# TensorE's order in the experts of a gated-DeltaNet, MLA and MoE block: written out by hand instead of left to the scheduler, with four token buffers and the final gain row loaded by DMA

## The chip, the cores and the metric

The kernel runs on one core of a Trainium2 chip. The metric is the device time of one execution in microseconds (us), the median of several executions. The profile is of one further execution, in which the hardware profiler recorded every instruction and every DMA packet.

## What is computed

One encoder block on 512 tokens of width 1024 in float32: two token mixers, their merge, and a mixture of 16 experts in which each expert picks its 64 best tokens. Cut to the part around the change, the reference is:

```python
def expert_choice_ffn(h, w_router, w_gate, w_up, w_down):
    cap = 64                                   # 2 * 512 // 16
    aff = softmax(h @ w_router)                # 512 x 16
    gate, idx = lax.top_k(aff.T, cap)          # each expert picks its tokens
    xe = h[idx]                                # 16 x 64 x 1024
    hid = silu(xe @ w_gate) * (xe @ w_up)      # each weight 1024 x 1024 per expert
    ye = (hid @ w_down) * gate
    return zeros_like(h).at[idx].add(ye)       # scattered back onto the tokens

x = x + gt2 * expert_choice_ffn(rms_norm(x, g_ffn) * (1 + sc2) + sh2, ...)
return rms_norm(x, g_final)
```

The gate, up and down weights of the 16 experts are 48 matrices of 4 MiB, 201 MB in all, each read once from HBM.

## The kernel before

The first two thirds of the program (both token mixers, their merge, the router with its top-64 selection) are not touched. The experts follow, from about 850 us on.

**Weights.** Each expert has three matrices m = 0 (gate), 1 (up), 2 (down), each cut into four quarters of 128 x 2048 floats. `order()` lists them as gate of e, down of e-1, up of e, for one expert after another; at the end stand gate and up of expert 15, down of expert 14 and down of expert 15, the last cut by columns into five pieces (three of 256 columns, two of 128; `last`). `load_quarters` (L988) issues their DMAs on SP in that order into a ring of 17 buffers `exw`; a quarter can be issued once TensorE has read the quarter 17 places before it.

**One expert.** `products(m, e, of)` runs the gate or up quarters: a quarter is four instructions in the program's order (two 128-row slices, two 64-column halves of the array) and eight records in the trace; they write the PSUM tiles `wg` and `wu`. `activated(e)` makes silu(gate) x up x score (ScalarE L1475, VectorE L1476). `turned(e)` transposes it on TensorE (tile `hTp`, L1482) and ScalarE copies it out. `down(e)` multiplies by the down quarters (tile `dnp`), and VectorE multiplies by the modulation row `gt2` into `ye` (L1505).

**Gather.** Tokens are gathered with one-hot matrices, four experts (a group) at a time: `group(g)` builds the one-hot `OG` on VectorE, and `gather(g, j0, n)` multiplies it by the token slices, which are split into a high and a low half (`xh` on ScalarE, `xl` on GpSimd); 16 matmuls for a pair of slices. The result goes to `XE[g]`, one tile `xe` of eight slices.

**Scatter.** `scatter(i, ye)` adds the outputs of a pair of experts i onto the tokens: for two column halves it splits `ye` into `yh` and `yl`, and for each of four token blocks runs two matmuls with the transposed one-hot `OHT` (made by `rows(i)`) into one of two PSUM tiles `sc`; VectorE adds the tile to the tokens (L1452). Eight such tiles a scatter. `gates(i)` collects a pair's scores with eight small matmuls.

**Order.** Up to the end of expert 14 the order of TensorE's instructions is set by the scheduler, from the order of the calls in the loop; the loop issues the scatter of the pair before, then `rows`, `group`, then the next expert's gate quarters, `turned`, `down` and the up quarters:

```python
        if e % 2 == 0 and i:
            scatter(i - 1, ye)
        if e % 4 == 3:
            group(e // 4 + 1)
        products(0, e + 1, range(3))
        turned(e)
        products(0, e + 1, [3])
        if e < NE - 2:
            down(e)
        products(1, e + 1)
```

**End.** The row `g_final` is loaded as 1 x 1024 and spread over the partitions by two matmuls with a row of ones (`spread`, L1318). Then come down of expert 14, and the five pieces of down of expert 15 in an order that is written by hand for TensorE, VectorE and ScalarE: matmuls of a piece, scatter of the piece before, adds, squares (`summed`), and GpSimd's multiplication by g_final (L1563, 16 instructions). After the last piece the row sums `rq` give the scale, and the tokens are scaled and stored.

Of the kernel before, what the change touches and what calls it, by code (L numbers as in the profile page):

```python
# [13 lines left out]
AF = mybir.ActivationFunctionType  # L14
# [8 lines left out]
NE = 16  # L23
# [17 lines left out]
def block_kernel(ctx: ExitStack, tc: tile.TileContext, x, c, positions, w_mod, b_mod, g_mix, w_in, conv_w,  # L41
# [1320 lines left out]
    def group(g):  # L1362

        o = wk_("OG", [4, 4, 64], F32R)
        e4 = slt[:, :, 4 * g:4 * g + 4][:, :, :, None].to_broadcast([128, 4, 4, 64])
        for h in (slice(0, 2), slice(2, 4)):
            dve.tensor_tensor(o[:, h], iot[:, None, None, :].to_broadcast([128, 2, 4, 64]), e4[:, h], op=OP.is_equal)
        XE[g] = wk_("xe", [8, 256])
        OG[g] = o
        if g:  # L1370
            for j in range(0, 8, 2):
                gather(g, j, 2)

    def gather(g, j0, n):

        ps = bank("mm")
        for j in range(n):
            hl_ = ahead.pop(j0 + j, None) if g == 0 else None
            hl_ = hl_ or halves_of(j0 + j)
            for t in range(4):  # L1380
                for v in range(2):
                    mm(ps[:, 256 * j:256 * j + 256], hl_[v][:, t], OG[g][:, t].rearrange("p e c -> p (e c)"),
                       t == 0 and v == 0, t == 3 and v == 1)
        for j in range(n):
            k = j0 + j
            a, b, v = sh_g[1][:, k:k + 1], sh_g[0][:, k:k + 1], ps[:, 256 * j:256 * j + 256]
            if k % 2:
                act.activation(XE[g][:, k, :], v, AF.Identity, bias=b, scale=a)
            else:
                dve.tensor_scalar(XE[g][:, k, :], v, a, b, op0=OP.mult, op1=OP.add)  # L1390

    def onehot(i):

# [59 lines left out]

    yb = []
    ssq = wk_("ssq3", [4, 5])
# [3 lines left out]
    def products(m, e, of=range(4)):  # L1459

        s_ = slice(64 * (e % 4), 64 * (e % 4) + 64)
        if (m, e) not in hid:
            hid[m, e] = bank(("wg", "wu")[m], 1, pe_)
        for hf in of:
            w = quarter(m, e, hf)
            for j in range(2 * hf, 2 * hf + 2):
                for q in range(2):
                    done = mm(hid[m, e][64 * q:64 * q + 64, :], XE[e // 4][:, j, s_],
                              w[:, j % 2].rearrange("p (a h b) -> p h a b", h=2, b=4)[:, q], j == 0, j == 7)
        return done  # L1470

# [6 lines left out]
    def turned(e):  # L1478
# [4 lines left out]
        hT_[e] = late[:, 0:512] if e == NE - 2 else wk_("sg_", 512)  # L1483
        act.activation(hT_[e], ps, AF.Copy)

    def lhid(e):
        return lambda j: hT_[e][:, 128 * (j % 4) + 64 * (j // 4):128 * (j % 4) + 64 * (j // 4) + 64]

    def down(e, middle=None):

        o_, lh, ps = slice(64 * (e % 2), 64 * (e % 2) + 64), lhid(e), bank("dnp", 1, pe_)
        for hf in range(4):
            if hf == 2 and middle:
                middle()
            w = quarter(2, e, hf)
            for j in range(2 * hf, 2 * hf + 2):
                for q in range(2):
                    done = mm(ps[64 * q:64 * q + 64, :], lh(j), w[:, j % 2, 512 * q:512 * q + 512], j == 0, j == 7)
        if e == 0:
            with tc.issue_after(done.ins):  # L1500
                spread(gt2, 0)
# [10 lines left out]
        done = products(m, 0, [hf])  # L1512
    gates(0)

    for e in range(NE - 1):
        i = e // 2
# [12 lines left out]
        turned(e)  # L1529
        products(0, e + 1, [3])  # L1530
        if e % 2 == 0:
            ye = wk_("ye", 1024)
# [9 lines left out]
    down(NE - 2, lambda: turned(NE - 1))  # L1542
# [3 lines left out]
    ctx.enter_context(tc.manual_schedule(engines={pe.engine, dve.engine, act.engine}))  # L1546

    def square(c, t, on):

# [88 lines left out]
```

## Time and profile before

| | |
|---|---|
| median of 3 runs | 1327.65 us (1326.37 to 1330.58) |
| the profiled execution's own time | 1334.39 us |
| its span, first to last instruction | 1332.5 us |
| mean granted TensorE clock | 0.977 of full |
| TensorE busy (matmul) | 1246.2 us, 94% |
| VectorE / ScalarE / GpSimd busy | 681.4 / 480.4 / 306.5 us |
| DMA moved | 333.17 MB, mean 250 GB/s |

The profiled execution took 1.9 us more than its span and 6.7 us more than the median of the runs. Busy shares are averages over stages with different limits; a table by stretches of time is read for the stage that the change touches. In the rows further down, PE is TensorE's matmuls, DVE VectorE, ACT ScalarE, POOL GpSimd, SP the queue that issues most DMAs; clock 1.00 is 2.4 GHz, 0.50 is 1.2 GHz.

### The profile page before, as it was taken

The numbers are of one execution on the slowest core, as the hardware profiler recorded it, in microseconds if no ns is written. First come the engines' busy times: TensorE is split into PE (matmuls) and PEld (weight loads), VectorE is DVE, ScalarE is ACT, GpSimd is POOL, SyncE is SP. The second block draws the span as 40 slices with busy tenths as digits, with TensorE's granted clock in tenths as the row PEclk, the third lists the DMA queues.
The fourth block names the chain that finished last, engine by engine and source line by source line (L and its number), as shares of the span: only waits on it lengthen the run. The fifth ranks groups of instructions, "written<-read, shape, count | busy, mean of one in ns | idle before, by whom it ended". The sixth has DMA issues, their size and how long they took to land.

```text
span 1332.5 us, 18305 instructions
## 1 busy us (share of the span) xinstructions
PE 1246.2 (94%) x6937; PEld 781.4 (59%) x6937; DVE 681.4 (51%) x1312; ACT 480.4 (36%) x993; POOL 306.5 (23%) x259
## 2 busy tenths in 40 slices
PE   6999999999998897999999999699999999999995
PEld 3767777666676675878877777333443443343334
DVE  4687766365679896535586766412131122212125
ACT  4466554456543334444542336411200110110013
POOL 2321200323444242444222243200200200110003
PEclk9999999999999898999999999799999999999998
DMA  9421213744453566677579673799999999999992
GB/s 352 140 60 44 80 48 99 234 138 135 138 162 96 173 166 187 181 231 187 175 250 333 221 288 127 288 380 421 420 420 421 420 421 420 421 420 421 421 388 76
DMA packets 153364, 333.17 MB, mean 250 GB/s; under 512 B 44545, under 2 KB 104143, under 8 KB 128316
## 3 DMA queue, kind: packets, MB, share of 16 engines
q1 hardware_dynamic: 129906, 308.23, 62.9%
q10 hardware_dynamic: 23034, 23.36, 5.6%
q8 instruction: 55, 0.90, 0.3%
q0 software_dynamic: 336, 0.41, 0.2%
q14 instruction: 33, 0.27, 0.1%
HBM read 307.83 MB, written 24.13 MB: 249 GB/s over the span
## 4 chain that ended last, share of the span: by engine, by line
PE 69%; DVE 16%; issue 5%; DMA 5%; ACT 3%; POOL 1%; SPq 0%; DVEq 0%; ACTq 0%; POOLq 0%
PE mm L88 23%; PE wg L88 9%; PE dnp L88 8%; PE wu L88 6%; PE po L88 5%; DVE pr L783 3%; PE lat L88 3%; PE sc L88 2%; DVE lanT L784 2%; PE s L88 2%; DMA wraw<-in_w_in_dram 1%; PE I L88 1%; PE pja L88 1%; PE S L88 1%; PE V L88 1%
## 5 line engine op out<-in xcount | busy, mean ns | idle before, releaser
L88 PE MATMUL mm<-hT,wh 128*128 128x512 f32 (+1 forms) x672 | 223.3, 409 | 0.0
L96 POOL TENSOR_TENSOR wl<-wraw,wh 128x512 fp32r<-128x512 f32 (+2 forms) x83 | 119.0, 1448 | 262.6 <-ACT wh L99 250.1
L88 PEld LDWEIGHTS mm<-hT,wh 128*128 128x128 f32 (+1 forms) x672 | 125.4, 190 | 44.2 <-issue 10.5
L99 ACT ACTIVATE wh<-wraw 128x512 fp32r<-128x512 f32 (+1 forms) x139 | 87.1, 650 | 137.8 <-PE mm L88 55.0
L88 PE MATMUL mm<-hT,wl 128*128 128x512 f32 (+1 forms) x336 | 135.7, 404 | 0.0
L88 PE MATMUL wg<-exw,xe 128*64 128x512 f32 x512 | 124.3, 603 | 1.3 <-DVE xe L1390 1.3
L1505 DVE TENSOR_TENSOR ye<-dnp,gt 64x512 f32<-64x512 f32 x30 | 20.7, 688 | 201.0 <-PE dnp L88 185.1
L88 PE MATMUL wu<-exw,xe 128*64 128x512 f32 x512 | 118.1, 596 | 0.0
L96 POOL TENSOR_TENSOR xl<-xs,xh 128x512 fp32r<-128x512 f32 x32 | 40.4, 1272 | 322.2 <-ACT xh L1358 258.1
L88 PEld LDWEIGHTS wu<-exw,xe 128*64 128x64 f32 x512 | 35.4, 137 | 67.0 <-issue 62.2
L88 PEld LDWEIGHTS mm<-hT,wl 128*128 128x128 f32 (+1 forms) x336 | 63.6, 189 | 15.8 <-DVE wl L96 0.6
L88 PEld LDWEIGHTS wg<-exw,xe 128*64 128x64 f32 x512 | 34.3, 137 | 58.9 <-issue 49.8
L96 DVE TENSOR_TENSOR wl<-wraw,wh 128x512 fp32r<-128x512 f32 (+1 forms) x56 | 47.2, 848 | 33.1 <-ACT wh L99 32.2
L783 DVE TENSOR_TENSOR pr<-lanT,nl 128x1 f32<-128x1 f32 (+30 forms) x62 | 56.7, 914 | 1.7
L1452 DVE TENSOR_TENSOR xa<-sc,xa 128x512 f32<-128x512 f32 x56 | 36.4, 686 | 31.2 <-PE sc L88 31.0
L88 PE MATMUL po<-W,am 128*128 128x512 f32 x192 | 50.1, 405 | 0.6 <-DVE W L96 0.6
L1358 ACT ACTIVATE xh<-xs 128x512 fp32r<-128x512 f32 x32 | 20.1, 629 | 70.6 <-PE sc L88 36.0
L660 DVE SCALAR_TENSOR_TENSOR cv<-mm,vecT,cv 128x510 f32<-128x510 f32 (+1 forms) x32 | 23.9, 748 | 39.7 <-ACT cv L656 39.1
L88 PE MATMUL mm<-oz,wh 128*128 128x512 f32 x128 | 40.3, 398 | 0.5 <-ACT wh L99 0.5
L88 PE MATMUL mm<-am,wh 128*128 128x512 f32 x128 | 40.7, 398 | 0.0
L88 PEld LDWEIGHTS po<-W,am 128*128 128x128 f32 x192 | 34.6, 188 | 10.4 <-issue 1.6
L1563 POOL TENSOR_TENSOR xa<-xa,late 128x256 f32<-128x256 f32 (+1 forms) x16 | 10.4, 686 | 118.2 <-ACT exw L1555 118.2
(599 smaller groups left out, 2435.5 us busy)
## 6 DMA issues: line engine op xcount, KB each, us to landing
exw<-in_w_gate_dram SPq DMA_DIRECT2D x64, 1024.0 KB
exw<-in_w_up_dram SPq DMA_DIRECT2D x64, 1024.0 KB
exw<-in_w_down_dram SPq DMA_DIRECT2D x63, 1024.0 KB
wraw<-in_w_in_dram SPq DMA_DIRECT2D x38, 512.0 KB
wm<-in_w_mod_dram SPq DMA_DIRECT2D x32, 512.0 KB
wraw<-in_w_in_dram ACTq DMA_DIRECT2D x16, 512.0 KB
xa<-in_w_mod_dram SPq DMA_DIRECT2D x16, 512.0 KB
kq<-kq_d SPq DMA_DIRECT2D x7, 1024.0 KB
```

Source lines behind the costliest of these rows:

```text
L88: return pe.matmul(o, lhsT, rhs, start=start, stop=stop)
L96: eng.tensor_tensor(o, a, b, op=OP.subtract)
L99: act.activation(hi, src, AF.Copy)
L660: dve.scalar_tensor_tensor(cv[:, -s:], ps[:, :512 + s], w(d), cv[:, -s:], op0=OP.mult, op1=OP.add)
L783: dve.tensor_tensor(pv, T3[:, 0:i, 0:i], nb, op=OP.mult)
L784: dve.tensor_reduce(T3[:, 0:i, i], pv, axis=AX.X, op=OP.add)
L1358: act.activation(xh, xs[:, j], AF.Copy)
L1452: dve.tensor_tensor(y[t][:, c:c + 512], ps, y[t][:, c:c + 512], op=OP.add)
L1505: dve.tensor_tensor(ye[o_, c], ps[64 * q:64 * q + 64, :], gt2[64 * q:64 * q + 64, c], op=OP.mult)
L1563: pool.tensor_tensor(y[t][:, cs], y[t][:, cs], gfin[:, cs], op=OP.mult)
```

## The change

TensorE's order is fixed by hand from expert 0 on. In an even iteration the eight tiles of the scatter stand one behind each quarter of the next expert's gate and of this expert's down. The gather of the next group stands, a pair of slices at a time, between the up quarters of the last expert of a group, and so `xe` becomes four tiles of two slices each, of which the first can be overwritten when the first up quarter has read it. `turned(e)` follows the third gate quarter. `rows` moves behind `down` of the even expert. The g_final row is read from HBM into all 128 partitions by one DMA of 512 KB, issued on SP behind the last piece of weights, in place of the two matmuls.

```diff
@@ group, gather
-        XE[g] = wk_("xe", [8, 256])
+        XE[g] = {}
         OG[g] = o
-        if g:
-            for j in range(0, 8, 2):
-                gather(g, j, 2)
...
+        if j0 // 2 not in XE[g]:
+            XE[g][j0 // 2] = wk_(f"xe{j0 // 2}", [2, 256])
@@ scatter
+        halves_ = []
         for c in range(0, D, 512):
             yh, yl = ...
             split(yh, yl, ye[:, c:c + 512])
+            halves_.append((c, yh, yl))
+        for c, yh, yl in halves_:
             for t in range(4):
...
                 dve.tensor_tensor(y[t][:, c:c + 512], ps, y[t][:, c:c + 512], op=OP.add)
+                yield
@@ down
-    def down(e, middle=None):
+    def down(e, between=()):
...
         for hf in range(4):
-            if hf == 2 and middle:
-                middle()
...
+            next(between, None)
@@ the loop over the experts
+    pe_order.enter_context(tc.manual_schedule(engines={pe.engine}))
     for e in range(NE - 1):
...
         activated(e)
-        if e % 2 == 0 and i:
-            scatter(i - 1, ye)
-        if e % 2 or e == NE - 2:
+        between = scatter(i - 1, ye) if e % 2 == 0 and i else iter(())
+        for k in range(4):
+            products(0, e + 1, [k])
+            next(between, None)
+            if k == 2:
+                turned(e)
+        if e < NE - 2:
+            if e % 2 == 0:
+                ye = wk_("ye", 1024)
+            down(e, between)
+        for _ in between:
+            pass
+        if e % 2 == 0:
             rows(i)
-        if e % 4 == 3:
-            group(e // 4 + 1)
-        products(0, e + 1, range(3))
-        turned(e)
-        products(0, e + 1, [3])
-        if e < NE - 2:
-            down(e)
-            if e % 2:
-                gates(i + 1)
-        products(1, e + 1)
-    sp.dma_start(gfin[0:1], g_final.rearrange("(o n) -> o n", o=1))
-    spread(gfin, 0)
-    spread(gfin, 1)
+        if e < NE - 2 and e % 2:
+            gates(i + 1)
+        if e % 4 == 2 and g < NE // 4:
+            group(g)
+        for k in range(4):
+            products(1, e + 1, [k])
+            if e % 4 == 2 and g < NE // 4:
+                gather(g, 2 * k, 2)
@@ before the five last pieces
+    load_quarters(parts.index((2, e, 0)), len(parts))
+    sp.dma_start(gfin, g_final.rearrange("(o n) -> o n", o=1).to_broadcast([128, 1024]))
```

How the rows of TensorE move. In the scatter of experts 6 and 7, before the change: `wu` are the up quarters of expert 8 (one row x4 is a quarter), `sc` the scatter's tiles.

```order
L88 MATMUL wu<-exw,xe 64x512 x4
L88 MATMUL sc<-yh,OHT 128x512
L88 MATMUL sc<-yl,OHT 128x512
L88 MATMUL sc<-yh,OHT 128x512
L88 MATMUL sc<-yl,OHT 128x512
L88 MATMUL sc<-yh,OHT 128x512
L88 MATMUL wu<-exw,xe 64x512 x4
L88 MATMUL sc<-yl,OHT 128x512
```

Two and a half tiles stand behind the first quarter, the rest behind the next ones. With the change, the same scatter (`wg` are the gate quarters of expert 9, `hTp` the transposes of expert 8):

```order
L88 MATMUL wg<-exw,xe_8712 64x512 x4
L88 MATMUL sc<-yh,OHT 128x512
L88 MATMUL sc<-yl,OHT 128x512
L88 MATMUL wg<-exw,xe_8746 64x512 x4
L88 MATMUL sc<-yh,OHT 128x512
L88 MATMUL sc<-yl,OHT 128x512
L88 MATMUL wg<-exw,xe_8780 64x512 x4
L88 MATMUL sc<-yh,OHT 128x512
L88 MATMUL sc<-yl,OHT 128x512
L1487 MATMUL hTp<-ident,sg__8937 128x128 x4
L88 MATMUL wg<-exw,xe_8814 64x512 x4
```

Each quarter now has one tile behind it (the other four stand behind the quarters of down), and the transposes have moved from the end of the up quarters to behind the third gate quarter. VectorE's rows for that scatter, with the change: `xa<-sc` are its adds, `sg` is the activation of expert 8, `ye<-dnp` the two halves of down's output.

```order
L96 TENSOR_TENSOR yl<-ye,yh 128x512 x2
L1481 SCALAR_TENSOR_TENSOR sg__8937<-wu,gate,sg__8937 128x512
L1456 TENSOR_TENSOR xa<-sc,xa 128x512 x7
L1515 TENSOR_TENSOR ye<-dnp,gt_7703 64x512
L1456 TENSOR_TENSOR xa<-sc,xa 128x512
L1515 TENSOR_TENSOR ye<-dnp,gt_7703 64x512
```

Both halves of `yl` stand ahead of the activation, and seven of the eight adds ahead of down's output. On SP, the end of the weights and the stores, with the change:

```order
L988 DMA exw<-in_w_down_dram 128x2048 x4
L988 DMA exw<-in_w_down_dram 128x8x256 x3
L988 DMA exw<-in_w_down_dram 128x8x128 x2
L1585 DMA late<-in_g_final_dram 128x1024
L1625 DMA out_dram<-xa 128x448
```

Before, g_final's row (`late<-in_g_final_dram 1x1024`) stood ahead of the four down quarters of expert 14.

## Rows read from the trace of the kernel before

**Rows 1.** Spans and granted clock of the cores.
```profile
core 0: 1332.5 us, clock 0.977
```
**Rows 2.** The page, the span in 40 slices of 33.3 us: DMA busy tenths, GB/s.
```profile
DMA  9421213744453566677579673799999999999992
GB/s 352 140 60 44 80 48 99 234 138 135 138 162 96 173 166 187 181 231 187 175 250 333 221 288 127 288 380 421 420 420 421 420 421 420 421 420 421 421 388 76
```
**Rows 3.** Busy time by stretches: PE, PEld, DVE, ACT, POOL, then clock, DMA share, GB/s.
```profile
850.00:860.00 10.00, 9.36 (x48) 5.11 (x48) 0.95 (x2) 3.25 (x6) 5.03 (x4) 0.88 0.45 165
880.00:890.00 10.00, 10.00 (x46) 3.67 (x47) 0.00 (x0) 1.16 (x2) 0.00 (x0) 1.00 0.99 413
1250.00:1260.00 10.00, 10.00 (x49) 3.43 (x50) 0.00 (x0) 0.60 (x1) 0.00 (x0) 1.00 1.01 420
```
**Rows 4.** The same view, the end of the weight stream.
```profile
1295.00:1298.00 3.00, 3.00 (x13) 1.27 (x14) 0.00 (x0) 2.75 (x4) 0.00 (x0) 0.68 1.02 315
...
1302.00:1303.00 1.00, 1.00 (x6) 0.29 (x4) 0.00 (x0) 0.00 (x0) 0.00 (x0) 1.00 0.02 4
1303.00:1304.00 1.00, 1.00 (x8) 0.29 (x4) 0.00 (x0) 0.00 (x0) 0.00 (x0) 1.00 0.00 0
```
**Rows 5.** Timeline of the end: start us, us, engine, line, operation [idle before <-releaser].
```profile
1293.12 1.98 PE L88 MATMUL mm<-late,ones 1*128 1x512 f32 x4
...
1295.71 8.78 PE L88 MATMUL dnp<-exw,late 128*64 128x512 f32 x32
...
1306.04 1.97 PE L88 MATMUL dnp<-exw,sg__9867 128*64 128x128 f32 x32 [1.54 <-issue]
...
1310.81 1.97 PE L88 MATMUL wu<-exw,sg__9867 128*64 128x128 f32 x32
...
1316.22 1.15 PE L88 MATMUL dnp<-exw,sg__9867 128*64 128x64 f32 x32
...
1323.05 0.17 DVE L1592 TENSOR_REDUCE rq<-ssq 128x4 f32<-128x20 f32 x1
```
**Rows 6.** Timeline, the same place four experts apart: up quarters begin.
```profile
1006.33 7.04 PE L88 MATMUL wu<-exw,xe 128*64 128x512 f32 x32
...
1123.84 4.46 PE L88 MATMUL wu<-exw,xe 128*64 128x512 f32 x20
```
**Rows 7.** Timeline of TensorE in one scatter (experts 6 and 7), up quarters of expert 8.
```profile
1094.51 1.89 PE L88 MATMUL wu<-exw,xe 128*64 128x512 f32 x8
...
1098.36 0.50 PE L88 MATMUL sc<-yh,OHT 128*128 128x512 f32 x1 [0.48 <-DVE xa L1452]
...
1105.57 0.50 PE L88 MATMUL sc<-yh,OHT 128*128 128x512 f32 x1 [0.32 <-DVE xa L1452]
...
1106.24 1.94 PE L88 MATMUL wu<-exw,xe 128*64 128x512 f32 x8
1108.11 0.50 PE L88 MATMUL sc<-yh,OHT 128*128 128x512 f32 x1
...
1109.03 0.63 PE L1482 MATMUL hTp<-ident,sg__8926 128*128 128x128 f32 x3 [0.19 <-DVE sg__8926 L1476]
```
**Rows 8.** Timeline of TensorE: transposes of expert 7, then the gather, which begins.
```profile
1070.19 0.75 PE L1482 MATMUL hTp<-ident,sg__8711 128*128 128x128 f32 x4 [0.91 <-DVE sg__8711 L1476]
...
1071.88 0.39 PE L88 MATMUL mm<-OG,xh 128*128 128x256 f32 x1
...
1074.10 1.08 PE L88 MATMUL wg<-exw,xe 128*64 128x512 f32 x4
```
**Rows 9.** Groups by line, 850 to 1333 us: busy us, mean ns, idle before.
```profile
L1563 POOL TENSOR_TENSOR xa<-xa,late 128x256 f32<-128x256 f32 (+1 forms) x16 | 10.4, 686 | 118.2 <-ACT exw L1555 118.2
L1600 ACT ACTIVATE xa<-xa,rq 128x896 f32<-128x896 f32 x2 | 2.0, 1034 | 0.3 <-DVE rq L1594 0.3
```
**Rows 10.** Busy time by stretches: TensorE with gaps, earlier in the program, columns of rows 3.
```profile
400.00:420.00 20.00, 16.84 (x74) 12.99 (x72) 19.55 (x31) 6.24 (x14) 8.45 (x5) 1.00 0.43 132
450.00:460.00 10.00, 7.04 (x21) 5.33 (x21) 5.80 (x11) 3.59 (x9) 4.26 (x5) 0.66 0.48 159
```

More of the change, by code (lines that the diff above doesn't have):

```diff
@@ L1367, in group @@
             dve.tensor_tensor(o[:, h], iot[:, None, None, :].to_broadcast([128, 2, 4, 64]), e4[:, h], op=OP.is_equal)
-        XE[g] = wk_("xe", [8, 256])
+        XE[g] = {}
         OG[g] = o
-        if g:
-            for j in range(0, 8, 2):
-                gather(g, j, 2)
     def gather(g, j0, n):
         ps = bank("mm")
+        if j0 // 2 not in XE[g]:
+            XE[g][j0 // 2] = wk_(f"xe{j0 // 2}", [2, 256])
+        xe = XE[g][j0 // 2]
         for j in range(n):
@@ L1387, in gather @@
             if k % 2:
-                act.activation(XE[g][:, k, :], v, AF.Identity, bias=b, scale=a)
+                act.activation(xe[:, k % 2, :], v, AF.Identity, bias=b, scale=a)
             else:
-                dve.tensor_scalar(XE[g][:, k, :], v, a, b, op0=OP.mult, op1=OP.add)
+                dve.tensor_scalar(xe[:, k % 2, :], v, a, b, op0=OP.mult, op1=OP.add)
     def onehot(i):
@@ L1467, in products @@
                 for q in range(2):
-                    done = mm(hid[m, e][64 * q:64 * q + 64, :], XE[e // 4][:, j, s_],
+                    done = mm(hid[m, e][64 * q:64 * q + 64, :], XE[e // 4][j // 2][:, j % 2, s_],
                               w[:, j % 2].rearrange("p (a h b) -> p h a b", h=2, b=4)[:, q], j == 0, j == 7)
@@ L1484, in turned, with turned_ @@
         act.activation(hT_[e], ps, AF.Copy)
+    def turned_(e):
+        yield
+        turned(e)
+        yield
     def lhid(e):
         return lambda j: hT_[e][:, 128 * (j % 4) + 64 * (j // 4):128 * (j % 4) + 64 * (j // 4) + 64]
-    def down(e, middle=None):
+    def down(e, between=()):
+        between = iter(between)
         o_, lh, ps = slice(64 * (e % 2), 64 * (e % 2) + 64), lhid(e), bank("dnp", 1, pe_)
         for hf in range(4):
-            if hf == 2 and middle:
-                middle()
             w = quarter(2, e, hf)
@@ L1513, in block_kernel @@
     gates(0)
+    pe_order = ctx.enter_context(ExitStack())
+    pe_order.enter_context(tc.manual_schedule(engines={pe.engine}))
     for e in range(NE - 1):
-        i = e // 2
+        i, g = e // 2, e // 4 + 1
         if e == NE - 2:
@@ L1521, in block_kernel @@
         activated(e)
-        if e % 2 == 0 and i:
-            scatter(i - 1, ye)
-        if e % 2 or e == NE - 2:
-            rows(i)
-        if e % 4 == 3:
-            group(e // 4 + 1)
-        products(0, e + 1, range(3))
-        turned(e)
-        products(0, e + 1, [3])
-        if e % 2 == 0:
-            ye = wk_("ye", 1024)
-        if e < NE - 2:
-            down(e)
-            if e % 2:
-                gates(i + 1)
-        products(1, e + 1)
-    sp.dma_start(gfin[0:1], g_final.rearrange("(o n) -> o n", o=1))
-    spread(gfin, 0)
-    spread(gfin, 1)
+        between = scatter(i - 1, ye) if e % 2 == 0 and i else iter(())
[3 more added lines that the diff above has]
+            if k == 2:
+                turned(e)
+        if e < NE - 2:
[5 more added lines that the diff above has]
+        if e % 2 == 0:
+            rows(i)
+        if e < NE - 2 and e % 2:
[6 more added lines that the diff above has]
+                gather(g, 2 * k, 2)
+    ye = wk_("ye", 1024)
     activated(NE - 1)
-    down(NE - 2, lambda: turned(NE - 1))
+    down(NE - 2, turned_(NE - 1))
     e, i, o_ = NE - 1, NE // 2 - 1, slice(64, 128)
@@ L1545, in block_kernel @@
     act.activation(ssq[:, 0, 0:1], lh(0)[:, 0:1], AF.Sqrt, bias=eps1, scale=0.0)
-    ctx.enter_context(tc.manual_schedule(engines={pe.engine, dve.engine, act.engine}))
+    ctx.enter_context(tc.manual_schedule(engines={dve.engine, act.engine}))
     def square(c, t, on):
```

## The prediction

> **What bounds the kernel now.** I read the table by stretches first, not the busy shares of the page. From about 880 us the DMA engines are full: 413 GB/s, then 420, at a DMA share of 0.99 to 1.01 [rows 3], and the slices show 420 or 421 GB/s without a dip for some 400 us [rows 2]. Weights are nearly all of it. Before that stretch they are not full (165 GB/s at 850 us), since TensorE frees the ring's buffers slowly while it gathers for the first group.
>
> Four experts are 48 quarters of 1.049 MB, 50.3 MB, which at 420 GB/s take 119.8 us. TensorE passes the same place four experts later after 1123.84 - 1006.33 = 117.5 us [rows 6]. So both run at nearly the same pace, and TensorE, which starts behind with a full ring, catches up by only 2.3 us in four experts. That it never has to wait for a weight does not make it the bound, and that the DMA is full does not make the DMA the bound: what decides is who is late at the end. There the answer is in two rows. The weight stream ends between 1302 and 1303 us (4 GB/s in that stretch, none after it) [rows 4], and I take 1302.7; TensorE reads the last piece at 1316.22 [rows 5]. **TensorE is 13.5 us behind the data.** So it is TensorE's path that sets the end now, and the stream is a floor 13.5 us below it.
>
> From the second stretch on, the end is a chain by itself: from the third of the five last pieces (1310.81) to the end of the span (1332.5) it takes 21.7 us, in which VectorE is the busy one, and 12.2 us of that lie ahead of the row sums at 1323.05 [rows 1, 5].
>
> **What the change is worth on TensorE's path.** A block of 32 records takes 7.04 us [rows 6], so a quarter 1.76.
>
> - *Scatter.* Now it costs the time from 1094.51 to 1109.03 less four quarters: 14.5 - 7.0 = 7.5 us [rows 7]; in it TensorE waits for VectorE's adds (0.48 and 0.32 are shown), because two or three tiles come in a row and there are two PSUM tiles. With one tile behind each quarter a tile costs 0.67 us (1105.57 to 1106.24), and a quarter with a tile behind it 1.87 instead of 1.76 (1106.24 to 1108.11), so 0.78 a tile and 6.2 a scatter. Gain 1.3 us, two scatters in four experts: 2.6. VectorE's add of a tile has more than 2 us until its PSUM tile is used again, so its wait goes under the quarters.
> - *Transposes.* In two of four experts TensorE waits 0.9 us for the activation [rows 8]; behind the third gate quarter, 5 us later, it is long ready. Gain 1.8 in four experts. ScalarE's copy of the result has the fourth gate quarter, 1.76 us, as cover; without it, down would wait for it.
> - *Gather.* 17 matmuls take 1071.88 to 1074.10, 2.2 us [rows 8], and the same number runs after the change. In pieces of 16 between quarters a piece pays the quarter's 0.11 once more. The gain is that GpSimd's split of the next pair runs under a quarter; the loss is that each pair waits for buffers of the pair before. I take 0, between -1 and +1 us a group. The four token buffers themselves cost nothing: each is overwritten right behind the quarter that read it last.
> - *Rows, gates, SP's order of weights* are the same instructions in other places: 0.
> - *g_final.* Two matmuls (1.98 us) leave the path. They use one row of the array, and right after them the clock was granted at 0.68 for three us [rows 4], so that down of expert 14 took 8.78 us where such a block takes 7.04 [rows 5, 6]. Together 3.7 us.
>
> Four experts give 4.4 us; from the third expert, where the DMA fills, to the end there are about 3.3 times four: 14.5 us, and with g_final **18 us that TensorE could be earlier**. Bounds: 3.7 if the new places gain nothing, about 25 if the waits around the gather go too. It can use only 13.5 of it, then it waits for each quarter as it lands.
>
> **What the new floor gives.** The stream has the same bytes and starts with the same gathers, so I let it end at 1302.7 again. The last two pieces, 1.05 MB at 315 GB/s [rows 4], are 3.3 us, so the third has landed at about 1299.4. From there the chain of before runs again, since its 21.7 us are VectorE's and not the data's: 1299.6 + 21.7 = 1321.3. Counted from the last piece it would be 1302.7 + 16.3 = 1319.0, so the third decides. What is late next is **g_final**: its 512 KB stand on SP behind the last piece, 1.25 us at 420 GB/s, so they land at 1304.0; GpSimd's 16 multiplications need 10.4 us [rows 9], to 1314.4. The scale would be there at 1299.6 + 12.2 + 0.7 = 1312.5, and the second of ScalarE's two scalings of 1.03 us [rows 9], at 1313.6, now waits until 1314.4: 0.8 us. Before, GpSimd had the row early and this wait did not exist. The span becomes 1322.1, 10.4 us less than 1332.5 [rows 1]. The sum stands against the profiled execution, 1334.39, which lies 6.7 us above the median; I take the same 10.4 off the median, 1327.65: **1317.3 us**. About 0.3% (4 us) is what a measurement of this kernel can tell from no change.
>
> **The rivals.**
>
> *The stream is faster without the profiler.* The runs shown are 6.7 us shorter than the profiled one. If that lies in the stream, TensorE is 20 us behind in them and all 18 us count: 1327.65 - 18 = 1309.6. For it: the profiled run is above all three others. Against: nothing says in which stage it lost them. The Trainium skill (DMA: Bandwidth & Descriptors, Specifications) gives a fabric ceiling of 435 GB/s, above the 420 of the trace, and an HBM limit per core of about 358 GB/s, which this trace contradicts. By 435 a quarter would land 0.09 us sooner, an estimate from that page, and the profiled stream would end some 14 us earlier.
>
> *Only g_final pays.* The new places give nothing, because each tile now brings a change of shape on TensorE. Then 3.7 us remain: 1323.9. Against: the price of a tile between quarters is measured, 0.78.
>
> *The clock falls while TensorE waits for data.* In the new state a quarter takes 1.76 us of 2.5, so TensorE is idle a quarter of the time in blocks without a scatter. At 7.04 busy of 10 us the granted clock was 0.66, at 16.8 of 20 it was 1.00 [rows 10]. A block at 1.2 GHz takes 14 instead of 7, but then TensorE is busy throughout, and in mid-stream there is room. It costs where it meets the end: down of expert 14 begins with its first quarter, about 10 us ahead of its last, at 1281 to 1283, and ends 14.5 us later at 1297; after down's output (1.5 us) the first piece starts near 1299.5 and takes the 26.5 us that it took before (1306.04 to 1332.5 [rows 5]): 1326 and 0.8 for g_final, so 1322 as a median. The Trainium skill (TensorE: Matmul & The Clock Gate, HAM oscillation) describes matmuls that wait for DMA and so run at the low clock again and again. By that rule this rival, and not the forecast, is the normal outcome; the trace has both [rows 10], and its gaps there are longer than the 0.7 us that I expect.
>
> *Slower: the fixed order waits for VectorE.* TensorE can no longer take other work while a tile waits. VectorE works in order, and its adds stand behind the activation and, the eighth, behind down's output. If each of the 56 tiles of the seven scatters waited 0.48 us, as the one in rows 7, that would be 27 us against 18 gained, while the wait sits on a path that is 13.5 us above the floor: 1327.65 + 9 = 1336.5. From 0.32 us a tile on nothing is gained. Against: seven of eight adds stand ahead of down's output, and there are two PSUM tiles.
>
> **How the numbers follow.** Forecast 0.68, with a range of its own from 1314 (no wait for g_final, the third piece a little sooner) to 1321 (TensorE still 3 us behind). Faster stream 0.10, only g_final 0.08, clock 0.09, slower 0.05. Faster by over 0.3% is below 1323.7: forecast, faster stream, most of the clock's case and a third of g_final's, 0.87; within 0.3%: the rest of these two, 0.08; slower 0.05. The range 1310 to 1325 leaves out the slower case and the ends of the others.
>
> **What would show it.** Right: the stream ends at about 1302 again at 420 GB/s; TensorE's idle time in the second half of the experts is ended by DMAs of weights, and the last piece is read within 4 us of the end of the stream; no waits of scatter tiles for VectorE; the clock at 1.00 through down of expert 14; GpSimd's multiplications begin at about 1304 and end after the scale is ready. Wrong: TensorE still far behind the stream at the end, a clock below 1 in stretches between 1100 and 1300, or a stream that ends at another time.

## The result, and the profile after

The changed kernel took 1321.91 us (median of 12 runs, 1317.24 to 1327.13), the kernel before, run beside it, 1331.75 us (median of 12). The ratio is 0.9929, 95% interval 0.9908 to 0.995; two slow runs of the kernel before, of 1353.06 and 1422.91 us, are not in it. The prediction's 10.4 us of 1327.65 are 0.9922. The profiled execution took 1326.64 us.

Cores view of the changed kernel, for [rows 1], and the page's slices, for [rows 2]:

```profile
core 0: 1324.8 us, clock 0.977
```
```profile
GB/s 340 154 60 42 82 48 94 232 148 129 125 184 96 152 170 187 187 172 214 160 247 336 247 322 126 228 368 421 420 421 420 421 420 421 420 421 420 421 415 187
```

The span is 7.7 us shorter, not 10.4. The place to look is the start of the experts. The view of the tile `wg` gives the first and last start of the gate matmuls; first the kernel before, then the changed one:

```profile
L88 PE MATMUL wg<-exw,xe x512: 592/592/1116, 851.2 to 1285.7; 128*64 128x512 f32 x171
```
```profile
L88 PE MATMUL wg<-exw,xe x512: 592/592/645, 853.7 to 1275.0; 128*64 128x512 f32 x171
```

The first gate matmul ran at 851.2 us and at 853.7 us, behind a part of the program that the change does not touch. From there to the end of the span it is 1332.5 - 851.2 = 481.3 us before and 1324.8 - 853.7 = 471.1 us after: **10.2 us less**. This difference, called the experts' time from here on, is the measure in which single profiled executions can be compared, since the start alone moved between 844.3 and 857.1 us in the 14 kernels below.

TensorE's waits from 880 to 1290 us (engine, line, what it waited for: us in total, times, longest), before (left out: transposes waiting 0.9 us for the activation, five times, and shorter ones) and after:

```profile
PE sc L88 <- DVE xa L1452: 5.6, 14, 0.5
PE mm L88 <- POOL xl L96: 1.8, 3, 0.9
PE mm L1410 <- DVE gate L1404: 1.7, 2, 0.8
...
```
```profile
PE wg L88 <- DMA exw<-in_w_gate_dram: 2.3, 4, 0.7
PE dnp L88 <- DMA exw<-in_w_down_dram: 2.2, 4, 0.6
PE wu L88 <- DMA exw<-in_w_up_dram: 1.5, 4, 0.6
PE mm L88 <- DVE OG L1367: 1.0, 3, 0.4
PE sc L88 <- DVE xa L1456: 0.5, 2, 0.3
```

Before, TensorE waited for VectorE and GpSimd and never for a weight; now 6.0 of 7.5 us of its waits are ended by weights. The same in the busy time by stretches of the changed kernel (columns of [rows 3]), which answers to [rows 3] and [rows 4]:

```profile
1200.00:1210.00 10.00, 10.00 (x48) 3.35 (x46) 3.40 (x9) 0.67 (x2) 0.00 (x0) 1.00 1.02 423
1230.00:1240.00 10.00, 8.64 (x38) 2.26 (x34) 0.75 (x1) 0.00 (x0) 0.00 (x0) 1.00 1.01 419
1240.00:1250.00 10.00, 8.40 (x38) 2.59 (x36) 0.00 (x0) 0.60 (x1) 0.00 (x0) 1.00 1.02 420
1250.00:1260.00 10.00, 8.68 (x42) 2.91 (x40) 3.30 (x8) 1.86 (x3) 0.00 (x0) 1.00 1.01 419
1260.00:1270.00 10.00, 8.26 (x34) 2.33 (x34) 1.44 (x2) 0.00 (x0) 0.00 (x0) 1.00 1.02 426
1270.00:1280.00 10.00, 9.49 (x42) 4.46 (x42) 4.60 (x7) 1.40 (x3) 0.00 (x0) 1.00 1.01 419
1280.00:1290.00 10.00, 10.00 (x48) 3.16 (x44) 0.80 (x2) 0.39 (x1) 0.00 (x0) 1.00 1.01 410
1290.00:1300.00 10.00, 7.72 (x74) 4.38 (x74) 2.38 (x5) 2.59 (x4) 0.00 (x0) 1.00 1.05 334
...
1303.00:1304.00 1.00, 1.00 (x19) 0.83 (x16) 0.24 (x2) 1.00 (x6) 0.00 (x0) 1.00 0.92 327
1304.00:1305.00 1.00, 1.00 (x8) 0.88 (x8) 0.91 (x3) 0.56 (x3) 0.00 (x0) 1.00 0.25 91
1305.00:1306.00 1.00, 1.00 (x33) 0.98 (x32) 1.00 (x3) 0.59 (x4) 0.00 (x0) 1.00 0.06 25
```

The stream is as full as before. TensorE catches up with it at about 1233 us, is busy 83 to 87% of the time until 1270, and its clock stays at 1.00 (2.4 GHz). Its first and its last wait for a weight before the end's own chain (timeline):

```profile
1233.14 1.94 PE L88 MATMUL wu<-exw,xe 128*64 128x512 f32 x8 [0.25 <-DMA exw<-in_w_up_dram]
...
1265.61 1.94 PE L88 MATMUL wg<-exw,xe 128*64 128x512 f32 x8 [0.65 <-DMA exw<-in_w_gate_dram]
```

Behind it comes the scatter of the last even iteration, which has no down quarters: five of its eight tiles stand in a row behind the fourth gate quarter, and TensorE falls back so far that from there to the end it waits for weights only 0.7 us more. The stream's rows run to 1306 us, but the bytes behind 1303 are mostly those of g_final. By the DMA packets of the traces (the last two pieces alone have packets of 512 bytes there) the last weight landed at 1304.41 us, 1302.21 before: 450.7 and 451.0 us after the first gate matmul. In all eleven profiled kernels below with a full stream and no early load of g_final that stalls it, this is 450.3 to 452.5 us.

The end, for [rows 5] (timeline: start us, duration, engine, line, operation, idle before and what ended it):

```profile
1298.93 1.97 PE L88 MATMUL wg<-exw,sg__9874 128*64 128x128 f32 x32 [0.50 <-DMA exw<-in_w_down_dram]
...
1301.98 1.97 PE L88 MATMUL wu<-exw,sg__9874 128*64 128x128 f32 x32
...
1306.31 10.71 POOL L1581 TENSOR_TENSOR xa<-xa,late 128x256 f32<-128x256 f32 x16 [124.17 <-DMA late<-in_g_final_dram]
...
1307.24 0.98 PE L88 MATMUL dnp<-exw,sg__9874 128*64 128x64 f32 x26
...
1313.69 0.80 DVE L1571 SCALAR_TENSOR_TENSOR exw<-xa 128x128 f32<-128x128 f32 x1
...
1314.61 0.17 DVE L1612 TENSOR_REDUCE rq<-ssq 128x4 f32<-128x20 f32 x1
...
1315.93 2.17 ACT L1620 ACTIVATE xa<-xa,rq 128x896 f32<-128x896 f32 x2 [0.81 <-POOL xa L1581]
```

The second piece waits for its load; the third follows it without a wait. The last piece is read at 1307.24, 2.8 us behind the last weight's landing; before, by the same packets, it was 14.0. From the third piece to the end it takes 1324.8 - 1301.98 = 22.8 us, 21.7 before: GpSimd waits for g_final, and ScalarE's scaling waits 0.81 us for GpSimd.

Last, four experts of TensorE's time while it is still behind the stream, for [rows 6]. Up quarters begin, with the gather of a group behind each:

```profile
1056.83 1.94 PE L88 MATMUL wu<-exw,xe 128*64 128x512 f32 x8
...
1167.47 1.94 PE L88 MATMUL wu<-exw,xe 128*64 128x512 f32 x8
```

That is 110.6 us for four experts, 117.5 before: 6.9 us less.

### The profile page after: what moved, and what is told of

Same layout as the page of the kernel before. It is cut to its first block, busy times and chain, and to the rows that moved or that the text cites. A ratio compares the mean times of both kernels' runs of the same rounds, so it can differ in the third digit from the quotient of the medians.

```text
span 1324.8 us, 18313 instructions
## 1 busy us (share of the span) xinstructions
PE 1241.3 (94%) x6933; PEld 775.3 (59%) x6933; DVE 689.0 (52%) x1312; ACT 480.3 (36%) x991; POOL 307.7 (23%) x259
## 4 chain that ended last, share of the span: by engine, by line
PE 67%; DVE 14%; DMA 10%; ACT 3%; issue 2%; POOL 1%; SPq 0%; DVEq 0%; ACTq 0%; POOLq 0%
PE mm L88 23%; PE wg L88 8%; PE wu L88 7%; PE dnp L88 6%; PE po L88 5%; DMA exw<-in_w_down_dram 3%; DVE pr L783 3%; PE sc L88 2%; DMA exw<-in_w_gate_dram 2%; PE I L88 2%; PE s L88 2%; PE pja L88 2%; DVE lanT L784 2%; DMA exw<-in_w_up_dram 2%; PE S L88 1%
## 5 line engine op out<-in xcount | busy, mean ns | idle before, releaser
L88 PE MATMUL wg<-exw,xe 128*64 128x512 f32 x512 | 121.1, 600 | 3.6 <-DMA exw<-in_w_gate_dram 2.3
L1515 DVE TENSOR_TENSOR ye<-dnp,gt 64x512 f32<-64x512 f32 x30 | 20.6, 688 | 133.4 <-PE dnp L88 117.4
L88 PEld LDWEIGHTS po<-W,am 128*128 128x128 f32 x192 | 34.6, 188 | 10.4 <-issue 1.6
L88 PE MATMUL mm<-OG,xh 128*128 128x256 f32 x128 | 34.1, 304 | 2.8 <-DVE OG L1367 2.8
```

The lines of the kernel that those rows point to most:

```text
L88: return pe.matmul(o, lhsT, rhs, start=start, stop=stop)
L1515: dve.tensor_tensor(ye[o_, c], ps[64 * q:64 * q + 64, :], gt2[64 * q:64 * q + 64, c], op=OP.mult)
```

## The experiments

The theory: the change took TensorE's path ahead of a stream that was already full, and now the stream sets the end with TensorE in reserve. The times below are of one profiled execution each; the ratio to the kernel before is of several timed runs. The third piece's column ends where the third of the five last pieces is begun; what is left of the experts' time is the tail, which VectorE, GpSimd and ScalarE set.

| kernel | span, us | first gate matmul, us | from there to the third piece, us | experts' time, us | ratio, 95% interval |
|---|---|---|---|---|---|
| before | 1332.5 | 851.2 | 459.6 | 481.3 | |
| changed | 1324.8 | 853.7 | 448.3 | 471.1 | 0.9929 (0.9908 to 0.995) |
| order only | 1317.4 | 846.6 | 449.7 | 470.8 | 0.9898 (0.9872 to 0.9924) |
| g_final only | 1336.1 | 857.1 | 457.4 | 479.0 | 0.9967 (0.9945 to 0.9989) |
| changed, shorter stream | 1312.1 | 847.4 | 442.3 | 464.7 | 0.986 (0.9828 to 0.9892) |
| before, shorter stream | 1328.8 | 849.3 | 457.8 | 479.5 | 0.9971 (0.9949 to 0.9993) |
| transposes 3 times | 1320.6 | 848.7 | 449.2 | 471.9 | 0.9933 (0.9907 to 0.9958) |
| transposes 8 times | 1322.2 | 850.2 | 450.7 | 472.0 | 0.9961 (0.9944 to 0.9977) |
| transposes 15 times | 1334.9 | 848.3 | 465.5 | 486.6 | 1.0057 (1.0036 to 1.0077) |
| scatter together | 1323.3 | 851.6 | 449.0 | 471.7 | 0.9937 (0.9917 to 0.9956) |
| gather together | 1322.2 | 851.5 | 448.0 | 470.7 | 0.9931 (0.9905 to 0.9958) |
| both together | 1322.9 | 851.0 | 449.2 | 471.9 | 0.9937 (0.9912 to 0.9962) |
| g_final early, first try | 1326.2 | 848.8 | 456.1 | 477.4 | 0.9978 (0.9963 to 0.9992) |
| g_final early, second try | 1315.6 | 844.3 | 450.2 | 471.3 | 0.9913 (0.9892 to 0.9934) |

**Order only.**

```diff
-    sp.dma_start(gfin, g_final.rearrange("(o n) -> o n", o=1).to_broadcast([128, 1024]))
+    sp.dma_start(gfin[0:1], g_final.rearrange("(o n) -> o n", o=1))
+    spread(gfin, 0)
+    spread(gfin, 1)
     ye = wk_("ye", 1024)
```

> The changed kernel, but with g_final brought in as in the kernel before (one row, then two spreads on TensorE ahead of the last experts' work). Theory (order buys nearly all; the load stream sets the end, TensorE has some 6 us to spare at 1230 to 1300 us): the spreads' 3.7 us disappear in TensorE's waits for data, GpSimd's products no longer wait for 0.5 MB behind the last piece, so the time is that of the changed kernel within 2 us: ratio to the kernel before 0.990 to 0.995. Rival 1 (only the g_final part pays): ratio 0.999 to 1.001. Rival 2 (TensorE still sets the end): 3.7 us longer than the changed kernel, ratio 0.996.

0.9898, experts' time 470.8: the order alone, with its four token buffers, gives the whole gain. The time of rival 1 (no gain without g_final) is excluded. Against the expectation, the spreads are not hidden in TensorE's waits: they stand behind the last wait for a weight (timeline of this kernel):

```profile
1259.08 1.94 PE L88 MATMUL wg<-exw,xe 128*64 128x512 f32 x8 [0.64 <-DMA exw<-in_w_gate_dram]
...
1280.15 1.98 PE L88 MATMUL mm<-late,ones 1*128 1x512 f32 x4
...
1296.29 1.97 PE L88 MATMUL wu<-exw,sg__9881 128*64 128x128 f32 x32
```

The third piece comes 449.7 us after the first gate matmul, so 1.4 of the spreads' 1.9 us show there against the changed kernel. The tail is shorter by 1.7 us (1317.4 - 1296.29 = 21.1), as GpSimd has its row early. The two cancel.

**g_final only.** The kernel before, with the DMA in place of the row and the spreads.

```diff
-    sp.dma_start(gfin[0:1], g_final.rearrange("(o n) -> o n", o=1))
-    spread(gfin, 0)
-    spread(gfin, 1)
...
+    load_quarters(parts.index((2, e, 0)), len(parts))
+    sp.dma_start(gfin, g_final.rearrange("(o n) -> o n", o=1).to_broadcast([128, 1024]))
```

> The kernel before with the g_final part alone: the load of 128 rows behind the last pieces, no spreads; TensorE's order as before. Theory: TensorE stays behind the stream by some 10 us at the end and gains just the spreads' 3.7 us, perhaps less 2 us for GpSimd: ratio 0.997 to 0.999. Rival 1 (only this part pays): ratio 0.993, the whole gain. Rival 2 (TensorE still sets the end): as the theory.

0.9967, just below what was expected; the experts' time is 2.3 us shorter. TensorE reads the last piece at 1319.88, while the stream is nearly over at 1308 to 1309 us. The transposes that stood behind the spreads now wait for VectorE (timeline and stretches of this kernel):

```profile
1300.39 0.75 PE L1482 MATMUL hTp<-ident,sg__9839 128*128 128x128 f32 x4 [0.93 <-DVE sg__9839 L1476]
...
1319.88 1.15 PE L88 MATMUL dnp<-exw,sg__9860 128*64 128x64 f32 x32
```
```profile
1308.00:1309.00 1.00, 0.15 (x2) 0.00 (x0) 0.79 (x2) 0.00 (x0) 0.00 (x0) 1.00 0.18 70
```

TensorE is still nearly 12 us behind (the last weight's packets end at 1308.03). So the two parts don't add up: with the order in place, g_final's 2 to 4 us bring nothing more.

**A shorter stream, in both kernels.** TensorE's work is the same, three loads of 1.05 MB are gone. (The first quarter is multiplied in place of the other three, so expert 13's output is another.)

```diff
-    parts = order()
+    parts = [v for v in order() if v not in [(2, 13, k) for k in (1, 2, 3)]]
+    held = []
...
     def quarter(*part):
+        if part[:2] == (2, 13):
+            if part[2] == 0:
...
+                held.append(EQ.pop(part))
+            return held[0]
```

> The changed kernel with three of the four down quarters of expert 13 not loaded; its first quarter is multiplied in their place, so TensorE's work is the same and 3.15 MB, 7.5 us of the stream at 420 GB/s, are gone. (Expert 13's output is thereby left wrong, which changes no time.) Theory (the stream sets the end, and TensorE has 6 to 7 us of waits for data from 1230 us on): 5 to 7 us faster than the changed kernel, ratio to the kernel before 0.987 to 0.989. Rival 2 (TensorE still sets the end): the time of the changed kernel, ratio 0.993.

> The kernel before with the same three down quarters of expert 13 not loaded and the first multiplied in their place: TensorE's work is unchanged, the stream is 7.5 us shorter. Theory (TensorE, 13.5 us behind the stream at the end, sets the time): no change, ratio 0.999 to 1.001. Rival 3 (the stream or what hangs on it set the time already before, and the change pays in another way): 4 to 7 us faster, ratio 0.995 to 0.997.

The changed kernel follows the stream: 471.1 to 464.7, 6.4 of the 7.5 us, with a ratio a little under the forecast one. The kernel before hardly does: 481.3 to 479.5. Its ratio of 0.9971 missed what was expected and stands at the edge of rival 3 (0.995 to 0.997, the stream as the bound already before); its interval leaves both open. The trace decides. The last weight lands 443.3 us after the first gate matmul, 7.7 us sooner than before, and the third piece comes 1.8 us sooner; TensorE reads the last piece 20.0 us behind the stream, 14.0 before. And of those 1.8 us, 1.2 are waits for VectorE: the scheduler set the last scatter in another place, where none of its tiles waits. Rival 2, TensorE as the bound of the changed kernel, falls too.

**How much reserve TensorE has.** The four transposes are repeated in the iterations of experts 10 to 13, 3, 8 and 15 times.

```diff
-        for q in range(4):
+        for q in range(4 + (4 * 7 if 10 <= e < 14 else 0)):
+            q = q % 4
             pe.transpose(ps[:, 128 * q:128 * q + 128], SG[e].rearrange...
```

> The changed kernel with 6 us more work on TensorE: in the iterations of experts 10 to 13 the four transposes of the activations are done three times in place of once (8 more of 0.19 us in each of four iterations). Measured from the first gate matmul to the end of the span, which takes 481.3 us before and 471.1 us in the changed kernel. Theory (TensorE waits for data 8.8 us between 1230 and 1300 us, so it has that much to spare): 0 to 2 us longer, 471 to 473 us. Rival 2 (TensorE's work sets the end): 6 us longer, 477 us.

> The same with 21 us more work on TensorE: the four transposes done eight times in place of once in the iterations of experts 10 to 13. From the first gate matmul to the end, theory: 21 less the 8.8 us to spare, 12 us longer than the changed kernel (10 to 14), some 483 us, that is 2 us above the kernel before: TensorE sets the end again. Rival 2: the whole 21 us, 492 us. Rival 4 (far more room than the waits show): under 5 us longer, 476 us.

> The changed kernel with the four transposes done 15 times in place of once in the iterations of experts 10 to 13. In the run with 8 times, 112 more transposes took 12.9 us (0.115 us each, one behind another), and all of it was hidden; 224 more are 26 us. Theory (TensorE has some 13 us to spare in the changed kernel, so its path became 22 to 23 us shorter, not the 18 of the prediction): 26 less 13, 12 to 13 us longer than the changed kernel, 483 to 484 us from the first gate matmul to the end. Theory of the prediction (18 gained, 10 used, 8 to spare): 18 us longer, 489 us. Rival 4 (the extra work is hidden in any amount): 472 us.

The expectation for 3 times came true. Those for 8 and 15 times missed: 472.0 us and not 483, which is within rival 4 (under 476), and 486.6 us, between the two theories (483 to 484 and 489). The first two took the extra work too large. Four transposes show as 0.63 to 0.75 us, but most of it is the end of the last one; 32 in a row show as 4.14 and 60 as 7.53 us. Timeline of the runs with 8 and with 15 times:

```profile
1187.68 4.14 PE L1488 MATMUL hTp<-ident,sg__9446 128*128 128x128 f32 x32
```
```profile
1190.44 7.53 PE L1488 MATMUL hTp<-ident,sg__9474 128*128 128x128 f32 x60
...
1313.81 1.97 PE L88 MATMUL wu<-exw,sg__10098 128*64 128x128 f32 x32
```

So 8 times are some 13 us more in four iterations and 15 times are 27.1 us (four clusters of 7.41 to 7.53 less 0.63 to 0.75 each). The 13 us cost 0.9 us of the experts' time, and every wait for a weight is gone from TensorE's list; of the 27.1 us, 15.5 come through. But in both the tail is 1.5 to 1.7 us shorter, as TensorE is so late that g_final is there in time or nearly so. TensorE's own path is read at the third piece: 13 us more delay it by 2.4, 27.1 us by 465.5 - 448.3 = 17.2. The reserve is 27.1 - 17.2 = **9.9 us**, for work placed ahead of the last wait for a weight; work behind it finds little (the spreads above). TensorE's path is therefore 459.6 - 448.3 + 9.9 = 21.2 us shorter than before; the prediction had 18. The timed runs agree for 15 times (1.0057 less 0.9929 is 17 us) and are less clear for 8 times (4 us, with intervals that overlap). The waits for weights in the profile (6.0 us up to 1290) understate the reserve; the gaps from 1230 to 1300 us (8.8) come near it, though 1.5 of them are a wait for VectorE.

**Is it the spreading?** Scatter tiles one after another, gather pieces one after another, and both; all else as changed.

```diff
+        for _ in between:
+            pass
         for k in range(4):
             products(0, e + 1, [k])
-            next(between, None)
```
```diff
         for k in range(4):
             products(1, e + 1, [k])
-            if e % 4 == 2 and g < NE // 4:
-                gather(g, 2 * k, 2)
+        for k in range(4 if e % 4 == 2 and g < NE // 4 else 0):
+            gather(g, 2 * k, 2)
```

> The changed kernel with the eight scatter tiles of a pair of experts one after another ahead of the gate quarters, as in the kernel before; all else as changed. From the first gate matmul to the end, theory: TensorE again waits for VectorE's sums of two buffers, 2.6 us in four experts, 8.6 us in all, of which the 8.8 us to spare hide nearly all: 0 to 3 us longer than the changed kernel, 471 to 474 us, but its waits for data from 1230 us on shrink to 1 to 3 us. Rival 6 (the spread scatter alone is what bought the gain): 479 to 481 us, as before. Rival 7 (those waits don't come back, since the four buffers and not the places took them): 471 us with the waits for data unchanged.

> The changed kernel with the four gather pieces of a group one after another behind the four up quarters, in place of one behind each quarter; all else as changed. Theory: TensorE waits again for GpSimd's split or for the buffers, up to 1.5 us in each of three groups, and all of it lies under the 13 us to spare: 471 to 472 us from the first gate matmul to the end, no difference to the changed kernel. Rival 8 (the gather between quarters is what the gain needs): 475 us or more.

> The changed kernel with both undone that were undone one by one: the scatter tiles one after another ahead of the gate quarters and the gather pieces one after another behind the up quarters; the four token buffers, the place of the transposes and g_final as changed. By the matmuls' start-to-start times from 880 to 1290 us the scatter alone put back 4.9 us of TensorE's time and the gather alone 10.0, each of them hidden; the run with 26 us more work put the room at 10.9 us. Theory (the room is one sum for all): 14.9 less 10.9, 4 us longer than the changed kernel, 475 us from the first gate matmul to the end (474 to 476), and no waits for weights are left ahead of the last pieces. Rival 9 (each of them is hidden on its own account, so both are too): 471 to 472 us.

None of the three loses anything that can be measured. With the scatter together the waits for VectorE are back, 5.9 us, yet the waits for weights did not shrink as expected. The reason stands in the timeline. Scatter of experts 4 and 5 with its eight quarters and a set of transposes, up to the transposes of `OG` behind it; first the changed kernel, then the tiles together:

```profile
1035.72 1.89 PE L88 MATMUL wg<-exw,xe 128*64 128x512 f32 x8
1037.53 0.50 PE L88 MATMUL sc<-yh,OHT 128*128 128x512 f32 x1
...
1056.30 0.60 PE L1410 MATMUL mm<-ident,OG 128*128 128x128 f32 x4
```
```profile
1032.41 0.50 PE L88 MATMUL sc<-yh,OHT 128*128 128x512 f32 x1
...
1033.93 0.51 PE L88 MATMUL sc<-yh,OHT 128*128 128x512 f32 x1 [0.33 <-DVE xa L1456]
...
1053.02 0.66 PE L1410 MATMUL mm<-ident,OG 128*128 128x128 f32 x4
```

1056.30 - 1035.72 = 20.58 us spread, 1053.02 - 1032.41 = 20.61 together. What the tiles wait for VectorE when they stand together they lose to the changes of shape when they stand apart: over four experts, by start-to-start times, the tiles together take 1.5 us more and the quarters 1.5 us less. My figure of 4.9 us "put back" counted the tiles' share alone and missed that the quarters became cheaper. So the expectation for both together, 475 us, missed, and was wrong in its terms: 471.9 is the time of rival 9, and only the gather's share is real. Four experts take 110.6 us in the changed kernel, 111.1 with the scatter together (1053.61 to 1164.66), 113.1 with the gather together, where the pieces wait for GpSimd's split, 6.8 us in nine waits, and 113.4 with both. Waits of the last run, 880 to 1290 us:

```profile
PE mm L88 <- POOL xl L96: 7.0, 9, 0.9
PE sc L88 <- DVE xa L1456: 6.0, 21, 0.3
PE wu L88 <- DMA exw<-in_w_up_dram: 0.5, 1, 0.5
```

Three groups of 2.5 to 2.8 us fit into the reserve, and little is left of it (one wait of 0.5 us for a weight). Since the reserve hides each of these, the runs don't show which part of the order the gain needs.

**g_final early, to beat both.** A row of 4 KB and two spreads under TensorE's waits, instead of 512 KB behind the last piece.

```diff
-        if e == NE - 2:
+        if e == 11:
             late = wk_("late", 4096, tag="xs")
             gfin = late[:, 512:1536]
+            sp.dma_start(gfin[0:1], g_final.rearrange("(o n) -> o n", o=1))
...
+        if e == 13:
+            spread(gfin, 0)
+            spread(gfin, 1)
```

> A kernel that may beat both: the changed kernel, with g_final as one row loaded at expert 11, when the buffer is free, and spread by TensorE in the iteration of expert 13, where TensorE waits for data. No 0.5 MB load behind the last pieces, no spread at the end. From the first gate matmul to the end, theory: GpSimd's products start with the first sums, and the end comes 21.7 us after the third piece has landed, as in the kernel before, not 22.8: 1 to 3 us shorter than the changed kernel, 468 to 470 us, ratio to the kernel before 0.987 to 0.992. Rival 5 (g_final's load is not in the way): the same as the changed kernel, 471 us.

Missed: its experts' time is 6.3 us longer than the changed kernel's. SyncE, which issues the weights in order, came to this DMA long before its buffer `xs` was free, and stood still (timeline of SyncE's queue, then a stretch):

```profile
1151.15 2.82 SPq L988 DMA_DIRECT2D exw<-in_w_gate_dram  x2
1177.13 0.25 SPq L1535 DMA_DIRECT2D late<-in_g_final_dram  x1
```
```profile
1170.00:1175.00 5.00, 5.00 (x34) 3.35 (x34) 0.64 (x2) 2.54 (x5) 2.90 (x3) 1.00 0.12 49
```

Some 23 us passed without an issue (1153.97 to 1177.13), 21.0 of them in a wait for GpSimd's split of the token slices, which read the buffer; the loads issued before lasted until about 1170, then the DMA engines ran dry at 49 GB/s. The last weight landed 458.7 us after the first gate matmul, 8.0 later than in the changed kernel, and the third piece came 7.8 us later: in a kernel that is bound by its stream the gap is paid in full. The tail, with the row there early, gave 1.5 back. The second try loads the row at expert 13 and spreads it behind that iteration's up quarters.

> The early spread once more, without what stalled the weight stream in the first try (there SyncE waited for g_final's buffer, which was still read by the gather, and no weights were issued meanwhile): the row of g_final is loaded at expert 13, when the buffer has long been free, and spread by TensorE behind the up quarters of that iteration, under its waits for data. From the first gate matmul to the end of the span the kernel before takes 481.3 us, the changed one 471.1, the one with the order alone 470.8. Theory (stream sets the end; GpSimd's products should not come last): the end is 21.7 us behind the third piece, 469 to 470.5 us. Rival 5 (g_final's way is not in the chain that ends last): 471 us.

Experts' time 471.3, the figure of rival 5 and not the 469 to 470.5 expected; but the tail is shorter. The spreads, then TensorE, GpSimd and VectorE at the end:

```profile
1257.39 1.98 PE L88 MATMUL mm<-late,ones 1*128 1x512 f32 x4
...
1294.47 1.97 PE L88 MATMUL wu<-exw,sg__9881 128*64 128x128 f32 x32
...
1295.47 2.81 POOL L1584 TENSOR_TENSOR xa<-xa,late 128x256 f32<-128x256 f32 x4 [122.57 <-ACT exw L1576]
1298.52 7.58 POOL L1584 TENSOR_TENSOR xa<-xa,late 128x256 f32<-128x256 f32 x12 [0.23 <-ACT exw L1576]
...
1306.21 0.28 DVE L1574 SCALAR_TENSOR_TENSOR exw<-xa 128x128 f32<-128x128 f32 x1
```

TensorE starts the third piece at 1294.47 here, so the end comes 1315.6 - 1294.47 = 21.1 us later, 22.8 in the changed kernel. That third piece came 450.2 us after the first gate matmul, against 448.3, which took the 1.7 us back: in this execution the spreads, meant to go under TensorE's waits, stand behind the last of them (an up quarter at 1255.52), and TensorE waits for no weight from there to the end. Its median of 1319.14 us and that of the kernel with the order only (1319.11) lie below the changed kernel's, but the intervals overlap: that either beats it is likely, not shown.

## Why the prediction was right, and where not

**The bound: right.** "TensorE's path sets the end now, and the stream is a floor 13.5 us below it": of 7.5 us less stream the kernel before gains 1.8, the changed one 6.4. The last piece is read 2.8 us behind the stream's end, within the 4 that were named. The reserve has an end, though: behind 1265 us TensorE waits for weights only 0.7 us, and 1.9 us of work added there (the spreads of the kernel with the order only) cost 1.4.

**The floor: right, on a start that moved.** The end of the weights was forecast for 1302.7 and came at 1304.41, the third piece for 1299.6 and came at 1301.98; the first gate matmul was 2.5 us late. With the start taken out, 10.2 us stand against 10.4. That the third piece starts as its own load lands is not what the rows show: it follows the second without a wait, and the second is the one that waited, 0.50 us. The place came out right because the two lie so close. The 1317.3 itself was missed by 4.6 us, 4.1 of which are the base: the kernel before took 1327.65 in the three runs that the forecast stood on and 1331.75 beside the changed one.

**g_final at the end: right.** Forecast: it lands at 1304.0 and ScalarE waits 0.8 us for GpSimd. Measured: GpSimd starts on it at 1306.31, late by 2.3 us, and ScalarE waits 0.81 us. What the sum lacked is that VectorE's last squares are slowed by GpSimd at work beside them (below).

**What TensorE gains: too small, and in part for a wrong reason.** Four experts save 6.9 us, not 4.4. A scatter of 6.2 us was forecast and is measured: 20.58 less eight quarters of 1.73 (four take 1035.72 - 1028.80 = 6.92) and 0.56 of transposes is 6.2. But the step's reason, "one tile behind each quarter" with VectorE's adds under the quarters, is not what pays: tiles one after another cost the same. What the kernel before lost was neither form but a mixture, two or three tiles and half a tile between quarters [rows 7], with both the waits and the changes of shape. The other places taken at 0 were not 0. By start-to-start times over four experts the gather's matmuls fell from 9.5 to 8.4 us and those of gates from 2.72 to 1.97, where a transpose had waited 0.8 us for VectorE's copies; and the gather between the quarters is worth 2.5 us a group against pieces in a row. Against that, g_final's 3.7 and 3.3 times 6.9 would be 26.5 us, and some 21 were measured. Of the 3.7 for g_final 2.2 are real (third piece from 459.6 to 457.4): without the spreads the transposes behind them wait 0.93 us for VectorE. Nor is the low clock a fixed part of that price: behind the same spreads at 1280.15 in the kernel with the order only, it was granted at 1.00 from 1280 to 1300 us. And there are three gathers in the loop, not 3.3. What else is missing was not followed. None of this reached the time, since only some 11 us up to the third piece could be used.

**Rivals.** *Faster stream without the profiler*: its ground was 6.7 us between the profiled execution and the median of three runs; over 12 runs the median is 1331.75, 2.6 us below the profiled one, and the 1309.6 did not come. *Only g_final pays*: excluded by the run with the order alone. *The clock falls*: TensorE waited 0.2 to 0.7 us a time and was busy 83 to 87%, and the clock was granted at 1.00 in every stretch from 1200 to 1305 us shown above. The Trainium skill (TensorE: Matmul & The Clock Gate, HAM oscillation) has matmuls that run at the low clock again and again in a loop whose compute is shorter than its wait for DMA. Here the waits are far shorter than the quarters between them, so the rule does not bear on them, and the prediction was wrong to call this rival the normal outcome by it. *Slower, the fixed order waits for VectorE*: 0.5 us for the scatter's tiles up to 1290 us, not 27.

## What to carry to other kernels

When two resources run at nearly the same pace for hundreds of microseconds, compare when each is done and not how busy it is: the lag at the end (13.5 us here) is the most that work on the late one can bring, and a second saving on the same path adds nothing. To see how much a hidden engine has in reserve, add a known amount of work to it until the time moves, and read it at a point of its own path, not at the end of the program (9.9 us here, where the waits for weights showed 6.0 and the end of the span would say 11.6). A reserve has a place: the same engine hid 10 us of work ahead of its last wait for a weight, and 0.5 of 1.9 us behind it. And when a helper load shares the queue of a stream that sets the end, put it where its buffer has long been free: one early wait cost 6 us here.

## What was not expected of the hardware

- **VectorE beside GpSimd.** A square and sum of 128x128 takes 0.28 us on VectorE when GpSimd is idle (second early try, at 1306.21, GpSimd done at 1306.10) and 0.37 to 0.80 when GpSimd multiplies (changed kernel, 1311.24 to 1313.69). VectorE's adds from PSUM of the same stage were not slowed: 0.68 to 0.69 us for 128x512 before GpSimd starts at 1306.31 and behind it. The Trainium skill (GPSIMD Engine Reference, Specifications) says that the two share their SBUF interfaces, with contention for VectorE's instructions that have two SBUF inputs, such as these squares; the rows agree, and the price here is a factor of up to 2.9.
- **A change of shape on TensorE has a price.** Eight tiles apart and eight tiles in a row with three waits of 0.3 us take the same 20.6 us with their quarters.
- **The start of the experts moves** from 844 to 857 us between executions in the profiles of 14 kernels that share the code ahead of it; a difference of 0.3% between two spans is hidden in it.
